# A hybrid encoder block on one core: gate and up's block products take high and low activations as one operand, two weight sums come by adding DMAs, and up's halves are folded one tile per work item

## The chip, the core and the metric

The kernel runs on one core of a Trainium2 chip. TensorE (PE in the profile; PEld is its weight load) multiplies matrices, VectorE (DVE), ScalarE (ACT) and GpSimd (POOL) work on elements, and DMA queues move data between HBM and the core's memory SBUF; SP issues most of them, POOL the others. Matmul results lie in eight banks of PSUM. The engines run side by side and wait for each other by semaphores; each works through its own instructions in order. The metric is the device time of one run, in microseconds (us), with every input in HBM at the start and the output there at the end. All of it is one program.

## The reference

An encoder block for 512 tokens of width 2048: a norm, an input projection, Fourier mixing for one half of the heads and spatial gating for the other, an output projection, then a SwiGLU feed-forward network of width 5632, each with a residual, and a final norm. The change lies in the feed-forward network:

```python
D_MODEL = 2048
SEQ = 512
D_FF = (-(-8 * D_MODEL // (3 * 256))) * 256
...
    for l in range(DEPTH):
        ...
        x = x + jnp.concatenate([y_f, y_g], axis=-1) @ w_out[l]
        h2 = rmsnorm(x, norm_ffn[l])
        x = x + (jax.nn.silu(h2 @ w_gate[l]) * (h2 @ w_up[l])) @ w_down[l]
    return rmsnorm(x, norm_final)
```

All inputs are float32.

## The kernel before

**Products of two halves.** The matmuls take float32r, a rounded float32, so every operand is split in two such tiles: hi is the value rounded (a copy by ScalarE, L173), lo is what the rounding left (value minus hi, by VectorE, L174). A product of two operands is then three matmuls, hi by hi, hi by lo and lo by hi, added up in PSUM.

**Stages.** Input projection and mixing first, then the output projection, then the feed-forward network: 4 of the 44 tiles of 128 ffn features by plain units (GateUp), 32 by block products (Block), the last 8 by plain units again, mixed with the products of the down projection (Product, Last), and at the end the last quarter of the down projection with the final norm.

**Block products.** Two neighbouring ffn tiles, p, are one Matrix for gate (named gb with its p) and one for up (upb). Its weights are four blocks of 1024 columns, 11, 12, 21 and 22 (half of the 2048 inputs, one or the other ffn tile). The tokens are halved as well (H = 256). By Strassen's scheme in Winograd's form the four products of halves are seven instead of eight. Each of the seven is a Block item with number i; sums of weights (Block.sums) and sums of activations (forms, made once in Forms) go in, and sums of the products come out (Block.out). The seven come in the order

```python
    ORDER = (1, 6, 2, 7, 5, 4, 3)
```

An item's matmuls are eight times (one for each of 8 input tiles j) the three of mm3b, each with 128 weight columns as the loaded operand and 256 tokens as the streamed one, all into one half of a PSUM bank:

```python
    def mm3b(ps, lhs, rhs, first, last):
        mm(ps, lhs[0], rhs[0], start=first, stop=False, skip_group_check=True)
        mm(ps, lhs[0], rhs[1], start=False, stop=False, skip_group_check=True)
        mm(ps, lhs[1], rhs[0], start=False, stop=last, skip_group_check=True)
```

There are 16 p, so 32 matrices, 224 items and 5376 such matmuls.

**What sets the order.** In drive the order of each engine is written by hand. While item k's matmuls run, the split of item k + 2 is made (prep), the weight sum of item k + 3 (sums), and the loads of later items are issued (load, by SP; a load waits until its tile's slot is free). Then come late and later, which hold the rest of the work of the one or two items before, then the item's matmuls (run) and the evacuation of its product (out). So VectorE's order in one item is: sum, split, late work, evacuation. A tile hi or lo has three buffers; a split can start when the item before has used its hi for the last time.

**Sums, evacuations and their end.** A matrix has four weight sums on VectorE (L633 to L639, 1024 columns each). Products 1 and 2 are copied out by ScalarE (L666, L670), the five others are added up by VectorE (L668 to L678, 256 columns each), into a tile o of the matrix, [128, 2, 512]. Behind gate's last item o is scaled by the norm (rg, L683), goes through tanh (L692, ScalarE) and becomes gate's silu (L697); behind up's last item, up's o is scaled (L685) and multiplied into gate's (L686), and keep stores the result in HBM (ad, by POOL, L527). The down stage reads it back.

**Slots.** Most tiles of 4 KB a partition come from one pool of 26 slots (slot). The sums of activations (hf) hold 16 of them through the block products; weight blocks go through the other ten. Pool w has three tiles each of raw, hi and lo.

## Time and profile before

| | us |
|---|---|
| three runs | 1849.55, 1850.15, 1850.8 (median 1850.15) |
| profiled execution | 1850.23 |
| its span, first to last instruction | 1848.5 |

The span by stages, cut at the first matmul of each (view by stretches; busy us of each engine, and the mean busy share of the 16 DMA engines):

| stage | us | TensorE | VectorE | ScalarE | POOL | DMA |
|---|---|---|---|---|---|---|
| projections and mixing | 485.74 | 481.27 | 240.92 | 193.65 | 53.02 | 0.36 |
| first 4 ffn tiles of gate and up | 88.52 | 88.36 | 63.66 | 31.68 | 0.84 | 0.37 |
| block products | 648.35 | 646.17 | 555.84 | 270.76 | 8.56 | 0.36 |
| down, last ffn tiles, final norm | 625.89 | 604.14 | 546.95 | 288.90 | 90.09 | 0.75 |

A row of an instruction group reads: line, engine, operation, tiles written and read, their sizes, count, then busy us and the mean ns of one, then the engine's idle time ahead of it and what ended it. A row of the order of time reads: start in us, length, engine, line, operation. The lengths of neighbouring instructions of one engine overlap (a matmul that lasts 0.28 starts 0.12 after the one before), so what one costs in a full queue is read from start to start.

### The profile page before, as it was taken

The numbers are of one execution on the slowest core, as the hardware profiler recorded it, in microseconds if no ns is written. First come the engines' busy times: TensorE is split into PE (matmuls) and PEld (weight loads), VectorE is DVE, ScalarE is ACT, GpSimd is POOL, SyncE is SP. The second block draws the span as 40 slices with busy tenths as digits, with TensorE's granted clock in tenths as the row PEclk, the third lists the DMA queues.
The fourth block names the chain that finished last, engine by engine and source line by source line (L and its number), as shares of the span: only waits on it lengthen the run. The fifth ranks groups of instructions, "written<-read, shape, count | busy, mean of one in ns | idle before, by whom it ended". The sixth has DMA issues, their size and how long they took to land.

```text
span 1848.5 us, 26416 instructions
## 1 busy us (share of the span) xinstructions
PE 1820.0 (98%) x10674; PEld 1614.0 (87%) x10674; DVE 1407.4 (76%) x1683; ACT 785.0 (42%) x1014; POOL 152.5 (8%) x160
## 2 busy tenths in 40 slices
PE   9999999999999999999999999999999999999996
PEld 7888888888888999999999999988888788788785
DVE  7554664333578888888888888889899898899957
ACT  6345533222333444443444444444445455444534
POOL 5001110000000000000000000001111111111104
PEclk9999999999999999999999999999999999999998
DMA  6322224442342343333334333338888878788672
GB/s 244 99 70 95 98 80 137 137 144 95 116 175 86 111 140 115 116 133 107 104 117 137 113 124 128 138 126 205 205 220 206 211 197 208 177 224 210 119 248 111
DMA packets 75577, 269.18 MB, mean 146 GB/s; under 512 B 8768, under 2 KB 8896, under 8 KB 75456
## 3 DMA queue, kind: packets, MB, share of 16 engines
q1 hardware_dynamic: 59616, 209.83, 33.7%
q0 software_dynamic: 15840, 57.68, 15.2%
q8 instruction: 83, 1.36, 0.3%
q14 instruction: 38, 0.31, 0.0%
HBM read 206.66 MB, written 60.82 MB: 145 GB/s over the span
## 4 chain that ended last, share of the span: by engine, by line
PE 89%; DVE 7%; issue 2%; ACT 1%; DMA 0%; POOL 0%; SPq 0%; ACTq 0%; DVEq 0%
PE upb L702 6%; PE upb L700 6%; PE upb L701 6%; PE gb L702 6%; PE gb L701 6%; PE gb L700 6%; PE d L790 5%; PE d L791 5%; PE d L789 5%; PE o L87 3%; PE o L85 3%; PE o L86 3%; PE g L87 2%; PE g L86 2%; PE g L85 2%; PE up L87 2%
## 5 line engine op out<-in xcount | busy, mean ns | idle before, releaser
L790 PE MATMUL d<-lo_d,X 128*128 128x512 f32 x560 | 219.4, 392 | 4.0 <-DVE lo_d L174 4.0
L789 PE MATMUL d<-hi_d,X 128*128 128x512 f32 x560 | 218.1, 389 | 2.4 <-DVE c L812 2.4
L791 PE MATMUL d<-hi_d,X 128*128 128x512 f32 x560 | 218.1, 389 | 0.0
L173 ACT CAST hi_d<-w 128x1024 fp32r<-128x1024 f32 x140 | 147.4, 1053 | 152.2 <-PE d L791 45.7
L174 DVE TENSOR_TENSOR lo_d<-w,hi_d 128x1024 fp32r<-128x1024 f32 x140 | 170.8, 1221 | 28.2 <-ACT hi_d L173 28.1
L173 ACT CAST hi_gb<-w_gb 128x1024 fp32r<-128x1024 f32 x112 | 117.5, 1049 | 150.0 <-PE upb L701 43.7
L173 ACT CAST hi_upb<-w_upb 128x1024 fp32r<-128x1024 f32 x112 | 117.5, 1050 | 135.4 <-PE gb L701 46.6
L174 DVE TENSOR_TENSOR lo_upb<-w_upb,hi_upb 128x1024 fp32r<-128x1024 f32 x112 | 136.8, 1221 | 37.3 <-ACT hi_upb L173 37.3
L174 DVE TENSOR_TENSOR lo_gb<-w_gb,hi_gb 128x1024 fp32r<-128x1024 f32 x112 | 136.7, 1221 | 34.4 <-ACT hi_gb L173 34.4
L702 PE MATMUL gb<-hf,lo_gb 128*128 128x256 f32 x512 | 145.0, 283 | 0.5 <-DVE lo_gb L174 0.5
L701 PE MATMUL gb<-hf,hi_gb 128*128 128x256 f32 x512 | 145.0, 283 | 0.4 <-DVE hf L174 0.4
L700 PE MATMUL gb<-hf,hi_gb 128*128 128x256 f32 x512 | 144.9, 283 | 0.0
L700 PE MATMUL upb<-hf,hi_upb 128*128 128x256 f32 x512 | 144.9, 283 | 0.0
L701 PE MATMUL upb<-hf,hi_upb 128*128 128x256 f32 x512 | 144.9, 283 | 0.0
L702 PE MATMUL upb<-hf,lo_upb 128*128 128x256 f32 x512 | 144.9, 283 | 0.0
L790 PEld LDWEIGHTS d<-lo_d,X 128*128 128x128 f32 x560 | 105.1, 188 | 30.8 <-DVE lo_d L174 9.3
L789 PEld LDWEIGHTS d<-hi_d,X 128*128 128x128 f32 x560 | 105.1, 188 | 25.1 <-ACT hi_up L173 2.0
L791 PEld LDWEIGHTS d<-hi_d,X 128*128 128x128 f32 x560 | 105.1, 188 | 21.3
L80 DVE TENSOR_TENSOR lo_o<-raw_o,hi_o 128x1024 fp32r<-128x1024 f32 x32 | 39.2, 1226 | 102.4 <-ACT hi_o L79 102.4
L700 PE MATMUL gb<-h2hi,hi_gb 128*128 128x256 f32 x384 | 108.8, 283 | 0.8 <-ACT t_gb L666 0.8
L702 PE MATMUL gb<-h2hi,lo_gb 128*128 128x256 f32 x384 | 108.8, 283 | 0.5 <-DVE lo_gb L174 0.5
L700 PE MATMUL upb<-h2hi,hi_upb 128*128 128x256 f32 x384 | 108.7, 283 | 0.0
(322 smaller groups left out, 4981.3 us busy)
## 6 DMA issues: line engine op xcount, KB each, us to landing
w<-in_w_down SPq DMA_DIRECT2D x80, 512.0 KB, 5.7
cd<-c POOLq DMA_DIRECT2D x80, 512.0 KB, 7.2
w_gb<-in_w_gate SPq DMA_DIRECT2D x64, 512.0 KB, 4.1
w_upb<-in_w_up SPq DMA_DIRECT2D x64, 512.0 KB, 4.4
raw_o<-in_w_out SPq DMA_DIRECT2D x32, 512.0 KB, 3.5
raw_g<-in_w_gate SPq DMA_DIRECT2D x24, 512.0 KB, 6.6
raw_up<-in_w_up SPq DMA_DIRECT2D x24, 512.0 KB, 6.8
ac<-ad SPq DMA_DIRECT2D x20, 512.0 KB, 3.6
```

The costliest lines, as they stand in the source:

```text
L80: nc.vector.tensor_sub(lo[:, c], raw[:, c], hi[:, c])
L85: mm(ps, lhs[0], rhs[0], start=first, stop=False)
L86: mm(ps, lhs[0], rhs[1], start=False, stop=False)
L87: mm(ps, lhs[1], rhs[0], start=False, stop=last)
L173: nc.scalar.copy(dst[0], src)
L174: nc.vector.tensor_sub(dst[1], src, dst[0])
L700: mm(ps, lhs[0], rhs[0], start=first, stop=False, skip_group_check=True)
L701: mm(ps, lhs[0], rhs[1], start=False, stop=False, skip_group_check=True)
L702: mm(ps, lhs[1], rhs[0], start=False, stop=last, skip_group_check=True)
L789: mm(p, X[:, 0, j, l], hi, start=j == 0 and not more, stop=False, skip_group_check=True)
L790: mm(p, X[:, 0, j, l], lo, start=False, stop=False, skip_group_check=True)
L791: mm(p, X[:, 1, j, l], hi, start=False, stop=j == 1, skip_group_check=True)
```

## The change

**Matmuls.** hi and lo of the activations now lie side by side in one tile (htile; forms). For each input tile j an item has two matmuls instead of three: the weights' hi streams hi and lo of the activations at once, 512 columns, hi by hi into the left half of the bank and hi by lo into the right; the weights' lo streams hi alone, 256 columns, into the left half. mm3b goes. The two halves of the bank are added when products leave: evacuations are 512 columns wide, and the last steps add halves.

**Weight sums.** Two of the four sums are made by DMA. Tiles w15 and w37 are loaded as 11 and 12 by SP, and POOL then issues a DMA that adds block 12 or 22 from HBM into the tile. Two sums stay on VectorE (L643, L645). A matrix has five slots of weights instead of four. The order of the seven products is BORDER.

**Evacuation.** Products 1, 5 and 2 are copied out by ScalarE, the others are added by VectorE, into two tiles o0 and o1 (one per ffn tile, halves apart). For gate, the halves are added into g (L694, two operations) and g is scaled (L695). For up, fold does it for one ffn tile at a time: add the halves (L703), scale (L704), multiply into g (L706). The first fold stands behind up's last item, the second in late, in the next item. o0, o1 and g take raw buffers of pool w; three raw units behind the stage take slots (early).

```diff
-    hpool = ctx.enter_context(tc.tile_pool(name="h", bufs=2 * KT))
+    hpool = ctx.enter_context(tc.tile_pool(name="h", bufs=KT))
...
     def htile(name):
-        return hpool.tile([P, S], F32R, tag="h", name=name)
+        t = hpool.tile([P, 2, S], F32R, tag="h", name=name)
+        return t[:, 0, :], t[:, 1, :], t
...
-            hi, lo = htile(f"h2hi{c}"), htile(f"h2lo{c}")
+            hi, lo, t = htile(f"h2_{c}")
             g = g_ffn[:, c : c + 1]
             nc.scalar.mul(hi, ps, g)
             nc.vector.scalar_tensor_tensor(lo, ps, g, hi, op0=ALU.mult, op1=ALU.subtract)
-            h2.append((hi, lo))
+            h2.append((hi, lo, t))
...
+    BORDER = (1, 5, 2, 6, 7, 3, 4)
...
                 t = slot(f"hf{j}_{i}", F32R, (P, 2, 2, H))
-                split(x[:, 2 * i : 2 * i + 2, :], (t[:, 0], t[:, 1]))
-                forms[fa, j], forms[fb, j] = ((t[:, 0, k, :], t[:, 1, k, :]) for k in range(2))
+                split(x[:, 2 * i : 2 * i + 2, :], (t[:, :, 0, :], t[:, :, 1, :]))
+                forms[fa, j], forms[fb, j] = t[:, 0], t[:, 1]
             for i, (k, c) in {1: (j, 0), 2: (KT // 2 + j, 0), 4: (KT // 2 + j, H)}.items():
-                forms[i, j] = both(h2[k], slice(c, c + H))
+                forms[i, j] = h2[k][2][:, :, c : c + H]
...
         def load(self):
             m = self.m
-            for k in {1: (11, 12, 22), 6: (21,)}.get(self.i, ()):
+            for k in {1: (11, 15), 5: (22,), 2: (21, 37)}.get(self.i, ()):
                 m.r[k] = slot(f"w{k}_{m.name}")
-                nc.sync.dma_start(m.r[k], m.src[k])
+                nc.sync.dma_start(m.r[k], m.src[{15: 11, 37: 12}.get(k, k)])
+                if k in (15, 37):
+                    nc.gpsimd.dma_start(m.r[k], m.src[12 if k == 15 else 22], accum_op=ALU.add)
 
         def sums(self):
             i, r = self.i, self.m.r
-            add, sub = nc.vector.tensor_add, nc.vector.tensor_sub
-            if i == 1:
-                add(r[12], r[12], r[22])
-            elif i == 6:
-                add(r[11], r[11], r[12])
-            elif i == 7:
-                add(r[21], r[21], r[11])
-            elif i == 5:
-                sub(r[11], r[11], r[22])
-        def behind(self, y):
-            return isinstance(y, Block) and y.m is self.m and (y.i, self.i) in ((1, 6), (2, 7))
+            if i == 6:
+                nc.vector.tensor_add(r[15], r[15], r[22])
+            elif i == 4:
+                nc.vector.tensor_add(r[21], r[21], r[15])
 
         def prep(self):
             i, r = self.i, self.m.r
-            self.split_weights(r[{1: 11, 6: 11, 2: 21, 7: 12, 5: 11, 4: 21, 3: 22}[i]], f"{self.m.name}_{i}")
+            self.split_weights(r[{1: 11, 5: 15, 2: 21, 6: 15, 7: 37, 3: 22, 4: 21}[i]], f"{self.m.name}_{i}")
 
         def run(self):
             m, i = self.m, self.i
             if i == 1:
-                m.o = slot(f"o_{m.name}", F32, (P, 2, S)) if m.up else wpool.tile([P, 2, S], F32, tag="raw", name=f"o_{m.name}")
-                m.t = small.tile([P, 3, H], F32, tag="t", bufs=1, name=f"t_{m.name}")
+                m.o = [wpool.tile([P, 2, 2, H], F32, tag="raw", name=f"o{f}_{m.name}") for f in range(2)]
+                m.t = small.tile([P, 2, S], F32, tag="t", bufs=1, name=f"t_{m.name}")
 
             more = i in (2, 3)
-            m.r["ps", i] = m.r["ps", {2: 1, 3: 5}[i]] if more else bank(f"{m.name}_{i}")
-            ps = m.r["ps", i][:, :H]
+            ps = m.r["ps", i] = m.r["ps", {2: 1, 3: 5}[i]] if more else bank(f"{m.name}_{i}")
             for j in range(KT // 2):
                 c = slice(j * P, (j + 1) * P)
-                mm3b(ps, (self.hi[:, c], self.lo[:, c]), forms[i, j], j == 0 and not more, j == KT // 2 - 1)
+                x = forms[i, j]
+                mm(ps, self.hi[:, c], x, start=j == 0 and not more, stop=False, skip_group_check=True)
+                mm(ps[:, :H], self.lo[:, c], x[:, 0, :], start=False, stop=j == KT // 2 - 1, skip_group_check=True)
 
         def out(self):
             m, i = self.m, self.i
-            ps, o = m.r["ps", i][:, :H], m.o
-            m1, u, w = (m.t[:, k, :] for k in range(3))
+            ps = m.r["ps", i]
+            u, w = m.t[:, 0, :], m.t[:, 1, :]
+            def o(f, t):
+                return m.o[f][:, t].rearrange("p a b -> p (a b)")
             if i == 1:
-                nc.scalar.copy(m1, ps)
+                nc.scalar.copy(u, ps)
+            elif i == 5:
+                nc.scalar.copy(o(1, 1), ps)
+            elif i == 2:
+                nc.scalar.copy(o(0, 0), ps)
             elif i == 6:
-                nc.vector.tensor_add(u, ps, m1)
-            elif i == 2:
-                nc.scalar.copy(o[:, 0, :H], ps)
+                nc.vector.tensor_add(u, ps, u)
             elif i == 7:
                 nc.vector.tensor_add(w, ps, u)
-            elif i == 5:
-                nc.vector.tensor_sub(o[:, 1, H:], ps, w)
-            elif i == 4:
-                nc.vector.tensor_add(o[:, 0, H:], ps, w)
+                nc.vector.tensor_sub(o(1, 1), o(1, 1), w)
+            elif i == 3:
+                nc.vector.tensor_sub(o(1, 0), ps, u)
             else:
-                nc.vector.tensor_sub(o[:, 1, :H], ps, u)
-                scale = rg.unsqueeze(1).to_broadcast([P, 2, S])
+                nc.vector.tensor_add(o(0, 1), ps, w)
                 if not m.up:
-                    pgu["o"] = o
+                    g = pgu["o"] = wpool.tile([P, 2, S], F32, tag="raw", name=f"g_{m.name}")
                     pgu["t"] = slot(f"th{m.p}", F32, (P, 2, S))
-                    nc.vector.tensor_mul(o, o, scale)
+                    for f in range(2):
+                        to = g[:, f, :].rearrange("p (a b) -> p a b", b=H)
+                        nc.vector.tensor_add(to, m.o[f][:, :, 0, :], m.o[f][:, :, 1, :])
+                    nc.vector.tensor_mul(g, g, rg.unsqueeze(1).to_broadcast([P, 2, S]))
                 else:
-                    nc.vector.scalar_tensor_tensor(o, o, 0.5, scale, op0=ALU.mult, op1=ALU.mult)
-                    nc.vector.tensor_mul(pgu["o"], pgu["o"], o)
-                    acts[m.p] = pgu["o"]
-                    keep(m.p)
+                    self.fold(0)
+        def fold(self, f):
+            halves = rg.rearrange("p (a b) -> p a b", b=H)
+            x = self.m.o[f][:, :, 0, :]
+            nc.vector.tensor_add(x, x, self.m.o[f][:, :, 1, :])
+            nc.vector.scalar_tensor_tensor(x, x, 0.5, halves, op0=ALU.mult, op1=ALU.mult)
+            to = pgu["o"][:, f, :].rearrange("p (a b) -> p a b", b=H)
+            nc.vector.tensor_mul(to, to, x)
 
         def late(self):
-            if self.i == 3 and not self.m.up:
+            if self.i == 4 and not self.m.up:
                 nc.scalar.activation(pgu["t"], pgu["o"], AF.Tanh, scale=0.5)
+            elif self.i == 4:
+                self.fold(1)
+                acts[self.m.p] = pgu["o"]
+                keep(self.m.p)
 
         def later(self):
-            if self.i == 3 and not self.m.up:
+            if self.i == 4 and not self.m.up:
                 o = pgu["o"]
                 nc.vector.scalar_tensor_tensor(o, pgu["t"], 1.0, o, op0=ALU.add, op1=ALU.mult)
-    def mm3b(ps, lhs, rhs, first, last):
-        mm(ps, lhs[0], rhs[0], start=first, stop=False, skip_group_check=True)
-        mm(ps, lhs[0], rhs[1], start=False, stop=False, skip_group_check=True)
-        mm(ps, lhs[1], rhs[0], start=False, stop=last, skip_group_check=True)
 
...
-            items += [Block(m, i) for i in ORDER]
+            items += [Block(m, i) for i in BORDER]
...
+        items[-1].early = n < 3
...
-    nc = bacc.Bacc("TRN2", target_bir_lowering=False, num_devices=1, dynamic_dma_scratch_size=8192)
+    nc = bacc.Bacc("TRN2", target_bir_lowering=False, num_devices=1, dynamic_dma_scratch_size=4096)
```

What moves on VectorE, at the end of an up and the start of the next gate. A name ends in the pair p, the product's number and a number of the build: lo_gb6_1_6025 is the low half of the weights of product 1 of gate, pair 6; gb6, upb5 in the place of a source are products in PSUM, t their running sums. In the program before, from up's second-last evacuation on:

```order
L676 TENSOR_TENSOR o_upb5_5874<-upb5_4_6029,t_upb5_5875 128x256
L174 TENSOR_TENSOR lo_gb6_6_6056<-w11_gb6_5833,hi_gb6_6_6055 128x1024
L678 TENSOR_TENSOR o_upb5_5874<-upb5_5_5998,t_upb5_5875 128x256
L685 SCALAR_TENSOR_TENSOR o_upb5_5874<-o_upb5_5874,rstdB_101 128x1024
L686 TENSOR_TENSOR o_gb5_5649<-o_gb5_5649,o_upb5_5874 128x1024
L174 TENSOR_TENSOR lo_gb6_2_6094<-w21_gb6_5871,hi_gb6_2_6093 128x1024
L637 TENSOR_TENSOR w21_gb6_5871<-w21_gb6_5871,w11_gb6_5833 128x1024
L639 TENSOR_TENSOR w11_gb6_5833<-w11_gb6_5833,w22_gb6_5837 128x1024
L174 TENSOR_TENSOR lo_gb6_7_6130<-w12_gb6_5835,hi_gb6_7_6129 128x1024
```

And in the changed one, from up's last evacuation on:

```order
L688 TENSOR_TENSOR o0_upb5_5503<-upb5_4_5649,t_upb5_5505 128x512
L703 TENSOR_TENSOR o0_upb5_5503<-o0_upb5_5503 128x2x256
L704 SCALAR_TENSOR_TENSOR o0_upb5_5503<-o0_upb5_5503,rstdB_101 128x2x256
L706 TENSOR_TENSOR g_gb5_5490<-g_gb5_5490,o0_upb5_5503 128x512
L643 TENSOR_TENSOR w15_gb6_5469<-w15_gb6_5469,w22_gb6_5500 128x1024
L176 TENSOR_TENSOR lo_gb6_2_5672<-w21_gb6_5528,hi_gb6_2_5671 128x1024
L703 TENSOR_TENSOR o1_upb5_5504<-o1_upb5_5504 128x2x256
L704 SCALAR_TENSOR_TENSOR o1_upb5_5504<-o1_upb5_5504,rstdB_101 128x2x256
L706 TENSOR_TENSOR g_gb5_5490<-g_gb5_5490,o1_upb5_5504 128x512
L176 TENSOR_TENSOR lo_gb6_6_5703<-w15_gb6_5469,hi_gb6_6_5702 128x1024
L176 TENSOR_TENSOR lo_gb6_7_5730<-w37_gb6_5530,hi_gb6_7_5729 128x1024
```

Before, two operations of 1024 columns stood between up's last evacuation (L678) and the split of product 2. Now the first fold and a sum stand between the last evacuation (L688) and that split, and the second fold stands between it and the split of product 6.

Behind a gate, from its last evacuation to the split of up's product 2, before:

```order
L678 TENSOR_TENSOR o_gb6_6100<-gb6_5_6223,t_gb6_6101 128x256
L683 TENSOR_TENSOR o_gb6_6100<-o_gb6_6100,rstdB_101 128x1024
L174 TENSOR_TENSOR lo_upb6_2_6318<-w21_upb6_6098,hi_upb6_2_6317 128x1024
L637 TENSOR_TENSOR w21_upb6_6098<-w21_upb6_6098,w11_upb6_6059 128x1024
L639 TENSOR_TENSOR w11_upb6_6059<-w11_upb6_6059,w22_upb6_6063 128x1024
```

And now:

```order
L688 TENSOR_TENSOR o0_gb6_5681<-gb6_4_5826,t_gb6_5683 128x512
L694 TENSOR_TENSOR g_gb6_5844<-o0_gb6_5681 128x512
L694 TENSOR_TENSOR g_gb6_5844<-o1_gb6_5682 128x512
L695 TENSOR_TENSOR g_gb6_5844<-g_gb6_5844,rstdB_101 128x1024
L643 TENSOR_TENSOR w15_upb6_5646<-w15_upb6_5646,w22_upb6_5675 128x1024
L176 TENSOR_TENSOR lo_upb6_2_5851<-w21_upb6_5706,hi_upb6_2_5850 128x1024
L176 TENSOR_TENSOR lo_upb6_6_5879<-w15_upb6_5646,hi_upb6_6_5878 128x1024
```

Where one scaling stood, two additions of halves, the scaling and a sum stand now.

POOL's queue in the stage held only one store for each pair before (ad<-o_gb, L527). Now, from pair 5 on:

```order
L638 DMA w15_upb5_5292<-in_w_up 128x1024
L534 DMA ad_3586<-g_gb4_5136 128x1024
L638 DMA w37_upb5_5354<-in_w_up 128x1024
L638 DMA w15_gb6_5469<-in_w_gate 128x1024
L638 DMA w37_gb6_5530<-in_w_gate 128x1024
L638 DMA w15_upb6_5646<-in_w_up 128x1024
```

Each pair has four adding loads now, and the store of a pair (g) stands ahead of the second adding load of the next pair's up, in the one queue.

More of the change, by code (lines that the diff above doesn't have):

```diff
@@ L131, in load_h @@
         xr = xrs[k // 2][:, k % 2, :]
-        hi, lo = htile(f"hhi{k}"), htile(f"hlo{k}")
+        hi, lo, _ = htile(f"h{k}")
         g = g_mix[:, k : k + 1]
@@ L508, in encoder_block @@
     class RawUnit(Item):
+        early = False
         def __init__(self, src, name):
@@ L514, in load @@
         def load(self):
-            self.raw = wpool.tile([P, U], F32, tag="raw", name=f"raw_{self.name}")
+            if self.early:
+                self.raw = slot(f"raw_{self.name}")
+            else:
+                self.raw = wpool.tile([P, U], F32, tag="raw", name=f"raw_{self.name}")
             nc.sync.dma_start(self.raw, self.src)
```

## The prediction

> **What bounds the kernel now.** First I read the page's chain of what ended last, by engine and by line, to see what carries the span.
>
> ```profile
> PE 89%; DVE 7%; issue 2%; ACT 1%; DMA 0%; POOL 0%; SPq 0%; ACTq 0%; DVEq 0%
> PE upb L702 6%; PE upb L700 6%; PE upb L701 6%; PE gb L702 6%; PE gb L701 6%; PE gb L700 6%; PE d L790 5%; PE d L791 5%; PE d L789 5%; PE o L87 3%; PE o L85 3%; PE o L86 3%; PE g L87 2%; PE g L86 2%; PE g L85 2%; PE up L87 2%
> ```
>
> The six lines of the block products (gb, upb) hold 36% of the chain, all on TensorE. So second comes the view by stretches: the stage that the change touches (574.26 to 1222.61, its first and its next stage's first matmul), and a stretch of the down stage to compare with.
>
> ```profile
> core 0: us, PE busy (x) PEld busy (x) DVE busy (x) ACT busy (x) POOL busy (x), PEclk, DMA share, GB/s
> 574.26:1222.61 648.35, 646.17 (x5377) 645.35 (x5376) 555.84 (x583) 270.76 (x307) 8.56 (x16) 1.00 0.36 120
> 1300.00:1700.00 400.00, 396.32 (x1731) 323.44 (x1730) 366.81 (x437) 191.95 (x243) 53.10 (x63) 1.00 0.81 204
> ```
>
> TensorE is never free in the stage, at full granted clock; VectorE is next with 86%. A matmul's own length in the profile (283 ns) overlaps its neighbour's, so the third view is the order of time, for the step from one start to the next, in the stage and at both ends of it:
>
> ```profile
> 504.68 0.39 PE L87 MATMUL up<-h2hi,lo_up 128*128 128x512 f32 x1
> ...
> 574.04 0.39 PE L87 MATMUL up<-h2hi,lo_up 128*128 128x512 f32 x1
> 574.26 0.28 PE L700 MATMUL gb<-h2hi,hi_gb 128*128 128x256 f32 x1
> ...
> 871.25 0.28 PE L700 MATMUL gb<-hf,hi_gb 128*128 128x256 f32 x1
> ...
> 874.13 0.28 PE L700 MATMUL gb<-h2hi,hi_gb 128*128 128x256 f32 x1
> ...
> 1222.49 0.28 PE L702 MATMUL upb<-hf,lo_upb 128*128 128x256 f32 x1
> 1222.62 0.40 PE L85 MATMUL g<-h2hi,hi_g 128*128 128x512 f32 x1
> ```
>
> From 504.68 to 574.04 lie 306 steps of 512 columns, 0.2267 us each. From 871.25 to 874.13, the first matmuls of two neighbouring products, lie 24 steps of 256 columns, 0.120 each. Where the two widths meet the steps are the same (0.22 for the 512 at 574.04, 0.13 for the 256 at 1222.49, in hundredths). The stage has 224 items of 24 matmuls: 5376 x 0.120 = 645.1, and the stretch is 648.35. So 3.2 us of waiting is in it, at its start.
>
> **The change part by part: TensorE.** The two steps differ by 256 columns and 0.1067 us, so 256 columns cost 0.1067; what is left of a step is 0.120 - 0.1067 = 0.0133 us, paid once for each matmul. An item had 8 x 3 x 0.120 = 2.880 us. Now it has 8 x (0.2267 + 0.120) = 2.773. Nothing else goes away: the columns stay, and one fixed share in three goes. 224 x 8 x 0.0133 = **23.9 us less**, if nothing is late.
>
> The Trainium skill, "TensorE: Matmul & The Clock Gate", section "Back-to-back issue gap", gives N / 2.4 + 2.5 ns for a warm matmul, 109 ns for 256 columns; by it 1792 removed matmuls would give only 4.5 us. The rows above speak against it with 120 and 227 ns.
>
> **VectorE's work.** These rows give its prices by width (and ScalarE's for a cast).
>
> ```profile
> L174 DVE TENSOR_TENSOR lo_gb<-w_gb,hi_gb 128x1024 fp32r<-128x1024 f32 x112 | 136.7, 1221 | 34.4 <-ACT hi_gb L173 34.4
> L173 ACT CAST hi_gb<-w_gb 128x1024 fp32r<-128x1024 f32 x112 | 117.5, 1049 | 150.0 <-PE upb L701 43.7 <-DVE w_gb L635 42.3 <-DVE w_gb L639 40.8
> L812 DVE TENSOR_TENSOR c<-d,uw 128x512 f32<-128x512 f32 x40 | 25.7, 684 | 0.0
> L637 DVE TENSOR_TENSOR w_gb<-w_gb,w_gb 128x1024 f32<-128x1024 f32 x16 | 19.6, 1225 | 0.5
> L672 DVE TENSOR_TENSOR t_gb<-gb,t_gb 128x256 f32<-128x256 f32 x16 | 6.8, 426 | 4.9 <-PE gb L702 4.9
> ```
>
> For one gate and its up (14 items): before, 14 splits and 8 sums and 4 final operations at 1.22, and 10 evacuations at 0.42, are 36.0 us against 14 x 2.880 = 40.3. After: 14 splits, 4 sums, the gate's scaling and its silu product at 1.22 (24.5), and at 0.684 eight evacuations of both halves, two subtractions into o1, two additions of halves and six operations of the folds (18 x 0.684 = 12.3): 36.8 us against 14 x 2.773 = 38.8. The four sums that the adding DMAs take over (4.9 us) are more than given back, and VectorE is nearly full. So its queue decides, and where operations overlap counts:
>
> ```profile
> 575.33 0.68 DVE L559 SCALAR_TENSOR_TENSOR s<-up,rstdB 128x512 f32<-128x512 f32 x1
> 576.04 0.69 DVE L560 TENSOR_TENSOR act<-act,s 128x512 f32<-128x512 f32 x1
> 576.65 0.69 DVE L595 TENSOR_TENSOR hr<-h2hi,h2lo 128x512 f32<-128x512 f32 x1
> ```
>
> ```profile
> 860.41 1.22 DVE L685 SCALAR_TENSOR_TENSOR o_upb<-o_upb,rstdB 128x1024 f32<-128x1024 f32 x1
> 861.66 1.22 DVE L686 TENSOR_TENSOR o_gb<-o_gb,o_upb 128x1024 f32<-128x1024 f32 x1
> 862.81 1.22 DVE L174 TENSOR_TENSOR lo_gb<-w_gb,hi_gb 128x1024 fp32r<-128x1024 f32 x1
> ```
>
> An operation that needs the result of the one ahead starts 0.71 (512 wide) or 1.25 (1024) after it; one that doesn't, 0.61 or 1.15. With these steps the 38 operations need some 35 of 38.8 us (20 x 1.15 and 18 x 0.61 to 0.71), so on the whole VectorE keeps up. It does not at two places, where its row of work is longest between a product's end and a split that TensorE needs. Two more views price them: how soon VectorE starts behind a product, and what a late split costs.
>
> ```profile
> 874.34 0.42 DVE L674 TENSOR_TENSOR o_gb<-gb,t_gb 128x256 f32<-128x256 f32 x1 [0.19 <-PE gb L702]
> ```
>
> ```profile
> 1391.34 1.22 DVE L174 TENSOR_TENSOR lo_g<-raw_g,hi_g 128x1024 fp32r<-128x1024 f32 x1
> 1392.19 0.39 PE L86 MATMUL g<-h2lo,hi_g 128*128 128x512 f32 x1
> 1392.61 0.50 PE L87 MATMUL g<-h2hi,lo_g 128*128 128x512 f32 x1
> 1392.95 0.39 PE L85 MATMUL g<-h2hi,hi_g 128*128 128x512 f32 x1
> ```
>
> VectorE started 0.21 after the next product's first matmul (874.13). The split that ended at 1392.56, 0.37 after the matmul ahead of its user, made two steps of 0.76 instead of 0.45, so it cost 0.30: a lo is free until 0.07 after that start.
>
> Behind an up (VectorE's first pair of orders above): 0.21 to the start, the last evacuation 0.71, first fold 0.71 + 0.71 + 0.61, sum 1.15, split 1.15, second fold 0.71 + 0.71 + 0.61, split of product 6 to its end 1.22: 8.50. TensorE needs it after three items, 3 x 2.773 + 0.07 = 8.39. Late by 0.11. The split of product 2 in the middle lands after 5.3, in time for 5.6. Behind a gate (the second pair): 0.21, evacuation 0.71, two additions 0.61 + 0.71, scaling 1.15, sum 1.15, split of product 2 1.22: 5.76 against 2 x 2.773 + 0.07 = 5.62. Late by 0.14. Sixteen pairs: 16 x 0.25 = **4.0 us more**. In the items that follow, VectorE has 1.2 to 3.1 us of work each and catches up, so lateness doesn't add up. The ends of this term are no lateness (0), and no overlap at all (every step 0.71 or 1.25: 8.90 and 6.06, late by 0.51 and 0.44, so 15.2 us).
>
> **ScalarE, loads and queues.** ScalarE copies three products of both halves instead of two of one; even at the 1.05 us of a cast of 1024 this is 3.2 us of a matrix's 19.4, and ScalarE's share of the stage above is 42%. Behind its copies stand the next casts, which need only the sum above to be done. The DMAs, by their time from issue to landing and by queue (packets, MB, share of 16 engines' span):
>
> ```profile
> cd<-c POOLq DMA_DIRECT2D x80, 512.0 KB, 7.2
> w_gb<-in_w_gate SPq DMA_DIRECT2D x64, 512.0 KB, 4.1
> ```
>
> ```profile
> q1 hardware_dynamic: 59616, 209.83, 33.7%
> q0 software_dynamic: 15840, 57.68, 15.2%
> ```
>
> Each matrix gains one plain load and two adding ones. The queues' shares give, for the 0.524 MB of one weight tile, 0.337 x 16 x 1848.5 / 209.83 x 0.524 = 25 us of engine time on SP's queue and in the same way 41 on POOL's, so 32 x 25 + 64 x 41 = 3424, over 16 engines and 648 us a share of 0.33 more: 0.36 becomes 0.69, below the 0.81 of the down stage, where the additions into HBM (cd) run beside VectorE's work already. An added weight waits for a slot, a plain load, POOL and the addition. By the order with its waits, w15's slot is freed 11 items (30 us) before it is split; 4.1 + 7.2 is 11.3. The trace shows no addition into SBUF: it is bounded by the plain 4.1 below and by twice the 7.2 above; I take 7.2, the only adding row, and nothing is paid at either end: 4.1 + 14.4 is still under 30. On POOL the addition for w37 of an up stands behind the store of the last pair, which waits for the second fold; from there 9 items (25 us) are left. The next gate's tile g waits for that same store, 5 items (14 us) later. SP's loads stand in line behind slots only, as before. Tiles that now hold hi and lo together, three raw units in slots, and the halved scratch of POOL's DMAs I cost at nothing: before the stage TensorE's and SP's orders are the same, and even one POOL transfer at a time would pass the down stage, 80 x 7.2 = 576 us in 626 (1222.62 to the end at 1848.5).
>
> **The sum.** The profiled execution took 1850.23 (span 1848.5), 0.08 above the median of the three runs. 1850.23 - 23.9 + 4.0 = **1830.3**. The 3.2 us of waits at the stage's start I leave, since VectorE's work there, the last forms and the first splits, stays.
>
> **The rivals.**
>
> (1) VectorE's queue behind a gate and an up is longer than I worked out, up to no overlap: 15.2 instead of 4.0, so 1841.5, and some us more if it slows beside the DMAs. For it: 36.8 of 38.8. Against: the overlapping starts above.
>
> (2) The change doesn't save what it says: most of the 13 ns belong to the columns, or come back in the mixed steps, and from 2.2 ns a matmul downwards (4.0 us over 1792) the late splits eat it all: 1850. Against: both mixed steps in the rows. By the rule of the Trainium skill's "TensorE: Matmul & The Clock Gate", section "Back-to-back issue gap", it would end in this rival.
>
> (3) Slower: operations on halves that lie 512 apart are slow. Eight of them stand in the two rows of work of a pair (the folds read or write halves). At the price of a full 1024 row each would cost 0.54 more, 8 x 0.54 x 16 = 69 us, so 1899; it decides from 0.16 us an operation (19.9 / 128). Against it a row with operands in pieces beside one without:
>
> ```profile
> L343 DVE SCALAR_TENSOR_TENSOR v<-vt 128x512 f32<-128x512 f32 x8 | 5.9, 740 | 10.9 <-ACT vt L342 10.7
> L392 DVE SCALAR_TENSOR_TENSOR v<-sv,g_sgu,bB 128x512 f32<-128x512 f32 x8 | 5.6, 745 | 0.0
> ```
>
> L392 takes its operands in four pieces and costs 5 ns more.
>
> **How the numbers follow.** Forecast 0.60 (1826 to 1835: lateness of 0 to 9 us); rival (1) 0.18 (1835 to 1846); rival (2) 0.10 (within 3.7 us of before, 0.2%, which is about what a measurement of this kernel can tell from no change); rival (3) and additions that land too late 0.12. The range takes the first two: 1826 to 1846. Faster by over 0.2%: 0.78; within: 0.10; slower: 0.12.
>
> **What would show it.** Right: 1792 fewer matmuls; items of 2.77 us with steps of 0.227 and 0.120; VectorE above 90% in the stage, waits of TensorE for lo alone, at product 2 behind a gate and product 6 behind an up, 0.1 to 0.2 each; DMA share near 0.7. Wrong: a pair of steps above 0.35, operations of L703 to L706 much above 0.69, waits for weights or for g.

## The result, and the profile after

| | us |
|---|---|
| changed kernel, four runs | 1837.7 to 1838.93, median 1838.1 |
| its span in the profiled execution | 1836.1 |
| kernel before, four runs | 1849.55 to 1850.8, median 1850.09 |
| ratio after to before | 0.9936, 95% interval 0.9922 to 0.995 |
| predicted | 1830.3, range 1826 to 1846 |

The kernel is faster by 12.0 us, 0.64%. The forecast was 19.9 us: the sign and the range hold, and the time is 7.8 us above the forecast. The range holds because it took in rival (1)'s band (1835 to 1846), and the experiments below show that rival (1)'s queue is not what put the time there.

The page of the changed kernel, its counts, its two DMA queues and its chain:

```profile
PE 1807.9 (98%) x8882; PEld 1519.1 (83%) x8882; DVE 1418.8 (77%) x1715; ACT 813.4 (44%) x1046; POOL 208.9 (11%) x224
...
q1 hardware_dynamic: 64224, 226.61, 35.5%
q0 software_dynamic: 25056, 91.24, 26.3%
...
PE 89%; DVE 7%; issue 2%; ACT 1%; DMA 1%; POOL 0%; SPq 0%; ACTq 0%; DVEq 0%
PE gb L663 11%; PE upb L663 11%; PE gb L664 6%; PE upb L664 6%; PE d L807 5%; PE d L808 5%; PE d L806 5%; PE o L89 3%; PE o L87 3%; PE o L88 3%; PE up L89 2%; PE up L87 2%; PE up L88 2%; PE g L89 2%; PE g L87 2%; PE g L88 2%
```

TensorE still holds the chain, now through two lines of the block products (L663 the 512-column matmul, L664 the 256-column one). The stage by the view of stretches, from its first matmul to the next stage's, and the same piece of the down stage as before:

```profile
core 0: us, PE busy (x) PEld busy (x) DVE busy (x) ACT busy (x) POOL busy (x), PEclk, DMA share, GB/s
574.30:1209.65 635.35, 633.36 (x3586) 549.92 (x3585) 566.71 (x612) 299.03 (x339) 61.63 (x77) 1.00 0.72 200
1300.00:1700.00 400.00, 396.32 (x1731) 323.39 (x1731) 365.49 (x436) 191.99 (x244) 51.85 (x61) 1.00 0.81 206
```

The stage went from 648.35 to 635.35 us, 13.0 less; the forecast for it was 621.2 + 3.2 + 4.0 = 628.4. So 6.9 of the missing 7.8 us are in this stage, with the clock at 1.00 and TensorE busy all the time. Behind the stage stand 1836.1 - 1209.65 = 626.4 us, 0.6 more than before.

Waits explain only a part of it. From the view of waits (engine and line, what it waited for, us in total, times, longest), first the waits of the matmuls in the whole stage, then those of the weight loads behind its start, from 590 on:

```profile
PE gb L664 <- DVE lo_gb L176: 1.1, 1, 1.1
PE gb L663 <- ACT t_gb L675: 0.9, 1, 0.9
...
PEld gb L664 <- DVE lo_gb L176: 1.0, 5, 0.2
PEld upb L664 <- DVE lo_upb L176: 0.7, 4, 0.2
```

The first two are at the stage's start. The recorded lengths of matmuls overlap, so the nine short waits show at the weight loads only. What is left is the length of the steps themselves. The order of time on TensorE shows the first matmul of neighbouring items in two parts of the stage, and in the middle an item whose low weights came late:

```profile
814.69 0.39 PE L663 MATMUL gb<-h,hi_gb 128*128 128x512 f32 x1
814.92 0.28 PE L664 MATMUL gb<-h,lo_gb 128*128 128x256 f32 x1
815.03 0.39 PE L663 MATMUL gb<-h,hi_gb 128*128 128x512 f32 x1
...
817.46 0.39 PE L663 MATMUL gb<-hf,hi_gb 128*128 128x512 f32 x1
...
820.23 0.39 PE L663 MATMUL gb<-h,hi_gb 128*128 128x512 f32 x1
...
823.01 0.39 PE L663 MATMUL gb<-hf,hi_gb 128*128 128x512 f32 x1
823.27 0.39 PE L664 MATMUL gb<-hf,lo_gb 128*128 128x256 f32 x1
823.50 0.39 PE L663 MATMUL gb<-hf,hi_gb 128*128 128x512 f32 x1
...
825.96 0.40 PE L663 MATMUL gb<-hf,hi_gb 128*128 128x512 f32 x1
...
854.26 0.40 PE L663 MATMUL gb<-h,hi_gb 128*128 128x512 f32 x1
...
857.08 0.40 PE L663 MATMUL gb<-hf,hi_gb 128*128 128x512 f32 x1
...
859.91 0.40 PE L663 MATMUL gb<-h,hi_gb 128*128 128x512 f32 x1
```

From 814.69 three items take 2.77 us each, as forecast. The item at 823.01 has its first low product 0.26 behind the first high one instead of 0.23, and the next step is 0.23 instead of 0.12. From 854.26 on, items of the same sixteen matmuls take 2.82 and 2.83 us, with no wait in them. To see the pattern, here are the times from each item's first matmul to the next one's, worked out from the starts in the trace (us; a row is one gate and its up, seven items each, and its number is the start of the row):

```
574.3   2.810 3.914 5.734 2.833 2.774 2.773 2.773 | 2.774 2.773 2.920 2.773 2.774 2.773 2.773
617.5   2.774 2.773 2.773 2.962 2.831 2.819 2.830 | 2.831 2.819 2.815 2.773 2.774 2.773 2.773
...
775.5   2.819 2.830 2.831 2.787 2.774 2.773 2.773 | 2.774 2.773 2.927 2.773 2.773 2.774 2.773
814.7   2.773 2.774 2.773 2.958 2.830 2.831 2.819 | 2.830 2.831 2.843 2.830 2.820 2.830 2.830
854.3   2.820 2.830 2.830 2.820 2.830 2.830 2.820 | 2.830 2.830 2.836 2.831 2.819 2.830 2.831
893.8   2.819 2.830 2.831 2.819 2.830 2.831 2.819 | 2.830 2.831 2.836 2.831 2.819 2.830 2.831
933.4   2.819 2.830 2.831 2.787 2.774 2.773 2.773 | 2.773 2.774 2.926 2.774 2.773 2.773 2.774
972.6   2.773 2.773 2.774 2.958 2.830 2.831 2.819 | 2.830 2.831 2.842 2.831 2.819 2.830 2.831
```

The alternating stream has **two beats**. In the fast one a pair of matmuls takes 347 ns (230 and 117). In the slow one the pairs take 361, 349 and 350 ns in turn (241 and 120, 236 and 113, 233 and 117), 353.3 on the mean. A beat lasts over many items and over both matrices. It changes at the fourth item of a gate (product 6), and once, in the row of 617.5, at the third of an up (product 2). Added up over the 224 items:

| us | forecast | measured |
|---|---|---|
| 224 items at 2.773 | 621.2 | 621.2 |
| start of the stage (first four items) | 3.2 | 4.2 |
| late low weights | 4.0 | 1.5 (9 items) |
| slow beat | 0 | 8.4 (156 items) |
| stage | 628.4 | 635.3 |

The row of late weights is what nine items took beyond 2.773; 0.2 us of it are slow steps behind five of the waits.

### The profile page after: what moved, and what is told of

Read it like the earlier page. It is cut to its first block, busy times and chain, and to the rows that moved or that the text cites. A ratio compares the mean times of both kernels' runs of the same rounds, so it can differ in the third digit from the quotient of the medians.

```text
span 1836.1 us, 23223 instructions
## 1 busy us (share of the span) xinstructions
PE 1807.9 (98%) x8882; PEld 1519.1 (83%) x8882; DVE 1418.8 (77%) x1715; ACT 813.4 (44%) x1046; POOL 208.9 (11%) x224
## 4 chain that ended last, share of the span: by engine, by line
PE 89%; DVE 7%; issue 2%; ACT 1%; DMA 1%; POOL 0%; SPq 0%; ACTq 0%; DVEq 0%
PE gb L663 11%; PE upb L663 11%; PE gb L664 6%; PE upb L664 6%; PE d L807 5%; PE d L808 5%; PE d L806 5%; PE o L89 3%; PE o L87 3%; PE o L88 3%; PE up L89 2%; PE up L87 2%; PE up L88 2%; PE g L89 2%; PE g L87 2%; PE g L88 2%
## 5 line engine op out<-in xcount | busy, mean ns | idle before, releaser
L663 PE MATMUL gb<-hf,hi_gb 128*128 128x512 f32 x512 | 181.8, 397 | 0.0
L663 PE MATMUL upb<-hf,hi_upb 128*128 128x512 f32 x512 | 181.4, 396 | 0.0
L664 PE MATMUL gb<-hf,lo_gb 128*128 128x256 f32 x512 | 144.3, 282 | 0.0
L664 PE MATMUL upb<-hf,lo_upb 128*128 128x256 f32 x512 | 143.7, 281 | 0.0
L663 PE MATMUL gb<-h,hi_gb 128*128 128x512 f32 x384 | 138.4, 399 | 0.9 <-ACT t_gb L675 0.9
L663 PE MATMUL upb<-h,hi_upb 128*128 128x512 f32 x384 | 137.6, 396 | 0.0
L835 POOL DMA_DIRECT2D cd<-c x80 | 68.8, 860 | 449.6 <-ACT c L825 163.3
L663 PEld LDWEIGHTS upb<-hf,hi_upb 128*128 128x128 f32 x512 | 96.1, 188 | 23.1
L663 PEld LDWEIGHTS gb<-hf,hi_gb 128*128 128x128 f32 x512 | 96.2, 188 | 22.6
```

The lines of the kernel that those rows point to most:

```text
L663: mm(ps, self.hi[:, c], x, start=j == 0 and not more, stop=False, skip_group_check=True)
L664: mm(ps[:, :H], self.lo[:, c], x[:, 0, :], start=False, stop=j == KT // 2 - 1, skip_group_check=True)
L835: nc.gpsimd.dma_start(cd[self.np_, to // 10 - 1, to % 10 - 1], c, accum_op=ALU.add)
```

## The experiments

After this table stood **theory A**: a wait for low weights throws the stream into the slow beat. Against it **B**: the transfers (share 0.72 of the DMA engines, before 0.36) slow TensorE down. And **C**: the alternation falls into the slow beat by itself.

**All high products first.** Product by product, the eight 512s and then the eight 256s:

```diff
             for j in range(KT // 2):
-                c = slice(j * P, (j + 1) * P)
-                x = forms[i, j]
-                mm(ps, self.hi[:, c], x, ...)
-                mm(ps[:, :H], self.lo[:, c], x[:, 0, :], ...)
+                mm(ps, self.hi[:, j * P : (j + 1) * P], forms[i, j], ...)
+            for j in range(KT // 2):
+                mm(ps[:, :H], self.lo[:, j * P : (j + 1) * P], forms[i, j][:, 0, :], ...)
```

> The changed kernel with each item's sixteen matmuls in another order: the eight of 512 columns first, then the eight of 256. Nothing else moves. The low weights are then wanted 8 x 0.227 - 0.227 = 1.6 us later in every item. Theory A (a matmul that had to wait for low weights, 0.15 to 0.19 us at product 6 behind an up, drops the mixed stream into a slower beat: triples of pairs 349, 350 and 361 ns instead of 347 each, which lasts over several matrices): no wait for low weights, no mixed beat, all items at 8 x 0.2267 + 8 x 0.120 = 2.773 us, the stage 621.2 + 4.2 at the start = 625.4 us against 635.35, the kernel about 1828 us. Theory B (the slow steps come from the transfers, now twice the bytes in SBUF per us): the order of the matmuls doesn't matter, items of 2.82 to 2.83 us remain, about 1836 us. Theory C (a 512 step behind a 256 step costs more at times, whatever was waited for): also 1828, and only a kernel without the wait in the old order tells it from A.

Measured: median 1829.18 us (four runs, 1828.58 to 1829.39), ratio to the kernel before 0.9888, interval 0.9875 to 0.9902, which lies wholly below that of the changed kernel. Its stage by the view of stretches, and two of its items in the order of time (eight equal matmuls in a row are one line there):

```profile
573.52:1200.48 626.96, 626.22 (x3585) 550.62 (x3584) 561.20 (x612) 299.41 (x340) 61.64 (x77) 1.00 0.73 202
```

```profile
694.89 2.00 PE L661 MATMUL gb<-hf,hi_gb 128*128 128x512 f32 x8
696.73 1.12 PE L663 MATMUL gb<-hf,lo_gb 128*128 128x256 f32 x8
697.68 2.00 PE L661 MATMUL gb<-h,hi_gb 128*128 128x512 f32 x8
699.52 1.11 PE L663 MATMUL gb<-h,lo_gb 128*128 128x256 f32 x8
700.48 0.86 PE L661 MATMUL gb<-hf,hi_gb 128*128 128x512 f32 x3
```

Every item behind the first three takes 2.793 us (694.89, 697.68, 700.48), with no wait and no slow beat. That is 0.020 more than forecast, because the 512s behind a run of 256s start at 235 ns a step and come down to 227 only towards the end of their run: 224 x 0.020 = 4.5 us. The start of the stage costs 626.96 - 224 x 2.793 = 1.3 us instead of 4.2, and the wait of 1.1 us for low weights in it is gone. This speaks against B: the transfers (0.73) were the same. A and C are still open.

**The merge alone undone.** Three matmuls of 256 columns per block again, all else as in the changed kernel:

```diff
-                mm(ps, self.hi[:, c], x, ...)
+                mm(ps[:, :H], self.hi[:, c], x[:, 0, :], ...)
+                mm(ps[:, H:], self.hi[:, c], x[:, 1, :], ...)
                 mm(ps[:, :H], self.lo[:, c], x[:, 0, :], ...)
```

> The changed kernel with the merge alone undone: three matmuls of 256 columns per product block again (24 per item), the rest of the change as it is. Theory A: items of 24 x 0.120 = 2.880 us throughout, no slower beat since no widths alternate, and the low weights no longer late (an item is 0.107 us longer than the forecast one); stage 645.1 + 4.2 = 649.3 us, the kernel about 1852 us, so the merge as such is worth 14 us and not 24. Theory B (transfers slow TensorE): items above 2.90 us, stage above 650. A rival on the rest of the change (folds, strided operations or adding transfers cost something by themselves): over 1853 us.

Measured: 1849.96 us, ratio to the kernel before 1.0002, interval 0.9993 to 1.0012. Its stage:

```profile
573.80:1221.31 647.51, 645.63 (x5378) 645.21 (x5376) 567.74 (x612) 299.64 (x339) 61.64 (x77) 1.00 0.72 197
```

All items behind the third take 2.880 us, so no low weight is late behind the start, and the share of the transfers is the same 0.72. So with items of this length adding transfers, folds, strided halves and the new order of products cost and bring nothing by themselves; the gain comes with the merge. Whether the merge would gain as much without the others was not tested. It is worth 11.9 us in the changed kernel's order and 20.8 us with the high products first.

**VectorE lightened by the fold.** Theories A and C differ where the order alternates and nothing is late.

```diff
         def fold(self, f):
-            nc.vector.tensor_add(x, x, self.m.o[f][:, :, 1, :])
-            nc.vector.scalar_tensor_tensor(x, x, 0.5, halves, op0=ALU.mult, op1=ALU.mult)
             nc.vector.tensor_mul(to, to, x)
```

> The changed kernel in its own order of matmuls; the two halves of up are not added and not scaled (two VectorE operations of each of the 32 fold calls are left out, so the values of act are others). VectorE then has about 1.4 us less to do before the low weights of product 6 behind an up. Theory A: the low weights of product 6 are in time, the stream never leaves its fast beat of 2.773 us; what is left is the wait at product 2 behind a gate, 16 x 0.15 = 2.4 us; stage 621.2 + 4.2 + 2.4 = 627.8 us, one time about 1830 us. Theories B and C: items of 2.82 to 2.83 us remain in most of the stage, 633 us or more.

Measured: one run of 1836.51 us, stage 633.86. My number was wrong. The slow beat is entered at a late weight, as A says. Its items from the third pair on:

```
655.1   2.773 2.774 2.773 2.773 2.774 2.773 2.773 | 2.774 2.773 2.927 2.773 2.773 2.774 2.773
694.0   2.773 2.774 2.773 2.773 2.774 2.773 2.773 | 2.774 2.773 2.952 2.830 2.830 2.820 2.830
733.3   2.830 2.819 2.830 2.831 2.819 2.830 2.831 | 2.819 2.830 2.847 2.831 2.819 2.830 2.831
```

Product 6 is in time everywhere and never changes the beat. At up's product 2 the first three waits (items of 2.920 to 2.927) leave the beat fast; the fourth (2.952) turns it slow, and it stays so to the end. The fourth wait is no longer than the others: its item's first two steps, from the trace, take 262 + 221 = 483 ns, those of the third 262 + 224 = 486. What its item takes longer are the slow steps behind the wait. So the length of a wait alone doesn't decide.

**Plain loads.** The same order with fewer transfers:

```diff
                 nc.sync.dma_start(m.r[k], ...)
-                if k in (15, 37):
-                    nc.gpsimd.dma_start(m.r[k], ..., accum_op=ALU.add)
```

> The changed kernel without its adding transfers (two per matrix; the sums of weights of products 5, 6, 7 and 4 miss one term each). The transfers of the stage fall by two fifths, VectorE and TensorE do all that they did. Theory A: nothing changes, low weights are late at the same two places, most items at 2.82 to 2.83 us, stage 635 us, one time about 1838 us. Theory B: items of 2.773 us throughout, stage about 627 us, 1830 us.

Measured: one run of 1836.33 us. Its stage:

```profile
574.06:1208.11 634.05, 632.08 (x3585) 548.55 (x3584) 566.68 (x612) 298.85 (x339) 8.57 (x16) 1.00 0.44 150
```

With the share of the transfers down from 0.72 to 0.44 the slow beat has the same steps, is entered at the same product (in the second pair) and takes as large a part (164 items, in the changed kernel 156). The 1.3 us less in the stage come from its start (2.6 us of waits instead of 4.2). B falls.

**No late weights in the alternating order.** The light fold, and gate's tile unscaled:

```diff
-                    nc.vector.tensor_mul(g, g, rg.unsqueeze(1).to_broadcast([P, 2, S]))
```

> The changed kernel's own order of matmuls, with VectorE lightened ahead of both late places: up's halves are neither added nor scaled, and gate's tile is not scaled (the values of act are others). The kernel without the fold's two operations stayed at 2.773 us per item for three matrix pairs, until a wait of 0.18 us at product 2 of the fourth pair, and was slow from there to the end. Theory A (only a wait for low weights puts the mixed stream into the slow beat): no wait is left at either place, so all items behind the first four at 2.773 us, stage 621.2 + 2.7 to 4.2 = 624 to 625.5 us, one time 1826 to 1828 us. Theory C (the mixed order falls into the slow beat by itself, sooner or later): items of 2.82 to 2.83 us appear without a wait ahead of them, stage above 628 us.

Measured: one run of 1828.04 us, stage 625.43. The stretch from the second pair's first matmul to the stage's end:

```profile
617.18:1199.56 582.38, 582.38 (x3362) 513.50 (x3361) 479.86 (x496) 279.40 (x316) 57.58 (x72) 1.00 0.74 204
```

These are 15 pairs, 210 items: 582.38 / 210 = 2.773 us, and no single item is off by more than 0.001. Its low weights were ready 1.28 us or more before their first use. So C falls as worded: left alone, the alternation keeps its fast beat for 582 us, beside transfers at 0.74.

**High products first at the two late places only** (product 6 of gate, product 2 of up), the rest alternating:

```diff
+            if (i, m.up) in ((6, False), (2, True)):
+                ...
+            else:
                 for j in range(KT // 2):
```

> Eight of 512 first and then eight of 256 only in the two items whose low weights are late (gate's product 6, up's product 2); the other twelve items of a pair alternate 512 and 256 as in the changed kernel. Theory A: the two waits are gone, the alternating items stay at 2.773 us and the two at 2.793: stage 621.2 + 32 x 0.020 + 2.7 to 4.2 = 624.5 to 626 us, the kernel about 1828 us, a little under the kernel with all items in that order (1829.2). Against it: if the step from an ordered item to an alternating one shifts the stream as a wait does, items of 2.82 to 2.83 us follow it and the time is 1830 to 1836 us.

Measured: 1836.78 us, ratio 0.9931, interval 0.9919 to 0.9944; stage 634.70. Behind its start no wait is listed in the stage, and each split of low weights ended 0.53 us or more before its first use, yet all alternating items from the first ordered one on take 2.82 to 2.83 us. So a wait isn't needed: a change of pattern puts the stream into the slow beat as well. The warning in the expectation came true, the forecast didn't.

**Low products one and two steps behind.**

```diff
+            n, lag = KT // 2, 1
+            for j in range(n + lag):
+                if j < n:
+                    mm(ps, self.hi[:, j * P : (j + 1) * P], forms[i, j], ...)
+                k = j - lag
+                if k >= 0:
+                    mm(ps[:, :H], self.lo[:, k * P : (k + 1) * P], forms[i, k][:, 0, :], ...)
```

> The alternating order with the low products one step behind: high 0, high 1, low 0, high 2, low 1 up to high 7, low 6, low 7. The low weights are wanted one 512 step, 0.227 us, later, more than the longest wait seen (0.19 us). Theory A: no wait, items of 2.773 us or a little above (each item has one pair of equal neighbours at each end), stage 621.2 + 4 = 625 us, the kernel about 1828 us. If the equal neighbours shift the stream into the slow beat by themselves: items of 2.82 us, stage 635 us, 1838 us.

> The same with the low products two steps behind, so that the low weights are wanted 0.45 us later than in the changed kernel. Theory A: as with one step, about 1828 us, and if one step left a wait of a few hundredths at some items, this one leaves none. If the shift at the ends decides: slow items as with one step.

Measured: one step behind 1836.71 us (ratio 0.993, 0.9917 to 0.9942), stage 635.46, items of 2.818 and 2.822 in turn. Two steps behind 1832.74 us (0.9908, 0.9895 to 0.9922), stage 629.80, items of 2.788, 2.813 and 2.806 in turn. No late weights behind the start of the stage in either (ready 0.35 and 0.53 us ahead, or more); orders with equal neighbours at an item's ends have slower steps without a wait. The forecasts of 1828 were wrong.

**One disturbance, and three, in a stream without late weights.** The kernel of the fifth experiment, with one item form "one step behind" at chosen places:

```diff
+            n, lag = KT // 2, int((m.p, m.up, i) == (6, 0, 1))
```

> The kernel without late weights (up's halves neither added nor scaled, gate's tile not scaled), all 224 items alternating but one: gate's product 1 of the fifth matrix pair has its low products one step behind (a 512 beside a 512 at its start, a 256 beside a 256 at its end). No wait comes with it. Theory A' (alternation keeps whichever beat its phase puts it in; anything that shifts the phase, a wait or two equal neighbours, changes the beat for good): 2.773 us per item up to that product, 2.82 to 2.83 from it to the end of the stage, 167 items x 0.054 = 9 us more than without the shift, stage 634 us, one time about 1837 us. Rival (the slow beat is tied to waits, or an item's disturbance ends with it): 2.773 us on both sides, stage 625 us, 1828 us.

> The same with that item form at three places: gate's product 1 of the fifth, ninth and thirteenth matrix pair. Theory A': the beat may change at each of the three and at no other place, so four stretches of constant beat; if every shift takes a fast stream to the slow beat and leaves a slow one slow, the stage is as with one shift (634 us); if a shift also takes a slow stream back, about 629 us. Rival: 625 us throughout.

Measured: one place 1827.57 us, stage 625.43: the disturbed item took 2.785 us, and the beat stayed fast on both sides. Three places 1833.26 us, stage 631.42: the first left the beat fast, the second turned it slow, the third left it slow. The second one in the order of time, with the first matmuls of the items around it (the disturbed item begins at 888.64 with two 512s):

```profile
885.87 0.40 PE L663 MATMUL upb<-h,hi_upb 128*128 128x512 f32 x1
...
888.64 0.62 PE L663 MATMUL gb<-h,hi_gb 128*128 128x512 f32 x2
...
891.46 0.40 PE L663 MATMUL gb<-hf,hi_gb 128*128 128x512 f32 x1
...
894.29 0.40 PE L663 MATMUL gb<-h,hi_gb 128*128 128x512 f32 x1
...
897.11 0.40 PE L663 MATMUL gb<-hf,hi_gb 128*128 128x512 f32 x1
```

2.77 us before, 2.82 and 2.83 behind, and so for the 111 items to the stage's end. That one disturbance is always enough was wrong. But the first one did change something. In both kernels the pairs behind it take 344 and 350 ns in turn (231 and 113, 233 and 117) where they took 347 each (230 and 117). The mean is the same, so the fast beat has two patterns; the second disturbance of the last kernel met the other pattern than the first. What holds in both kernels: the pattern changed only at a disturbance, and between two of them never.

## Why the prediction was right or wrong

**Right: the mechanism.** The profile has 10674 - 8882 = 1792 matmuls fewer, no wait for added weights or for g, and without the merge there is no gain (second experiment: ratio 1.0002).

**Right in the fast beat: the price of a removed matmul.** The kernel with no late weights kept 2.773 us per item, 0.107 less than 2.880, over 210 items: 13.3 ns for each removed matmul. The steps inside are 230 and 117 ns, not the 227 and 120 of equal neighbours; only their sum came out. The rule that the prediction weighed (the Trainium skill, "TensorE: Matmul & The Clock Gate", section "Back-to-back issue gap": N / 2.4 + 2.5 ns, there the gap of an isolated matmul) would have given 2.5 ns for each removed matmul; among equal neighbours 256 columns took 120.0 and 512 took 226.7, which is N / 2.4 + 13.3 ns in both rows.

**Wrong: "items of 2.773" as the price everywhere.** This is the term of 23.9 us, and it is the step that failed: it measured 23.9 - 8.4 = 15.5. The prediction took the mixed steps from the two places where 512 and 256 meet once, and took a sum of two single steps for the price of a stream. In 156 of 224 items part of the saving came back in the mixed steps, 0.054 us of 0.107 in a slow item. That is what rival (2) named ("come back in the mixed steps"), at half its price in a slow item. One pair in three of the slow beat takes 0.361 us, above the 0.35 that the prediction had named as a sign of being wrong. Nothing alternated in the kernel before, so it could not show the beat, but it did show dearer steps: behind the 256s at 1222.62 the first five 512s took 233, 236, 228, 233 and 231 ns, and the prediction had read only the one step ahead of them. So a bound was due, and the forecast's own 1826 to 1835 had none for it.

**The late low weights: places and sizes right, count wrong.** VectorE's work behind an up, in the order of time of the changed kernel:

```profile
817.68 1.22 DVE L643 TENSOR_TENSOR w_gb<-w_gb,w_gb 128x1024 f32<-128x1024 f32 x1
818.81 1.22 DVE L176 TENSOR_TENSOR lo_gb<-w_gb,hi_gb 128x1024 fp32r<-128x1024 f32 x1
819.95 0.68 DVE L703 TENSOR_TENSOR o_upb<-o_upb 128x512 f32<-128x512 f32 x1
820.67 0.69 DVE L704 SCALAR_TENSOR_TENSOR o_upb<-o_upb,rstdB 128x512 f32<-128x512 f32 x1
821.39 0.69 DVE L706 TENSOR_TENSOR g_gb<-g_gb,o_upb 128x512 f32<-128x512 f32 x1
822.01 2.35 DVE L176 TENSOR_TENSOR lo_gb<-w_gb,hi_gb 128x1024 fp32r<-128x1024 f32 x2
```

The last row is two splits, of products 6 and 7. The first ends at 822.01 + 1.22 = 823.23, that is 8.54 behind the matmul at 814.69; the prediction's sum was 8.50. The first two steps of a late item took 0.14 us more than a pair of the fast beat, at product 6 and at product 2; forecast were 0.11 and 0.14. (The whole item took 0.185 more at product 6, since slow steps followed.) But only nine items had such a wait, not 32: in the slow beat three items take 0.16 us more, and the same chain is then in time. So the term measured 1.5 instead of 4.0 (1.3 for the waits alone), and the slow beat paid for part of itself.

**Small terms.** The start of the stage cost 4.2 instead of the unchanged 3.2; other kernels with the same matmul order there had 2.6 to 4.2, and why was not looked for. Outside the stage 0.6 us came on top; no experiment looked for it.

**Rivals (1) and (3).** VectorE was busy for 566.71 of 635.35 us, 89%, where I expected above 90; its queue overlapped as forecast. The strided folds take the forecast price (last column but the idle time: mean ns):

```profile
L706 DVE TENSOR_TENSOR g_gb<-g_gb,o_upb 128x512 f32<-128x512 f32 x32 | 22.2, 692 | 1.1
L704 DVE SCALAR_TENSOR_TENSOR o_upb<-o_upb,rstdB 128x512 f32<-128x512 f32 x32 | 22.1, 692 | 1.1
L703 DVE TENSOR_TENSOR o_upb<-o_upb 128x512 f32<-128x512 f32 x32 | 22.0, 689 | 0.5
```

**Transfers.** Share 0.72, forecast 0.69. The adding transfers by issue to landing:

```profile
w_gb<-in_w_gate POOLq DMA_DIRECT2D x32, 512.0 KB, 6.1
w_upb<-in_w_up POOLq DMA_DIRECT2D x32, 512.0 KB, 7.5
```

The estimate of 7.2, taken from the additions into HBM, holds for additions into SBUF, and nothing waited for them.

## What to carry to other kernels

Price a mixed stream of instructions by a mixed stream: two steps read at a single boundary don't say what hundreds of alternations cost, and where the trace has none, bound them. When a merge makes a tight engine faster, look for the operand that now comes last; here eight high products ahead of the eight low ones gave the low weights 1.6 us of slack and took the kernel from 1838.1 to 1829.2 us, most of it because the slow beat (8.4 us) has no place in that order. A merged kernel that gains less than its arithmetic can be read item by item: here equal items of unequal length, with no wait in them, showed that the stream itself had two beats, set off by small disturbances.

## What the runs showed of the hardware

- A stream of alternating float32r matmuls of 512 and 256 columns, each with its own weight load, ran here at 346.7 ns or at 353.3 ns a pair, at granted clock 1.00. It kept one beat for up to 582 us and changed it only in an item whose low split ended behind its first matmul, or at a change of pattern.
- The length of a wait doesn't decide alone. Behind the stage's start, where the fast beat met late weights, the first two steps of the item took 483 to 486 ns where it stayed fast (seven times in the changed kernel and the third experiment) and 490 to 494 where it turned slow (five times), but once 483 turned it slow as well.
- The way back goes by a few nanoseconds. In the changed kernel and the one with plain loads, slow items of product 6 whose low split ended 48 to 50 ns behind the item's first matmul turned the beat fast (six of six, in items of 2.787 or 2.788 us); where it ended 54 to 57 ns behind, the beat stayed slow (fifteen of fifteen). That goes together; no run moved that time by itself.
- The steps depend on the neighbours: 227 ns for a 512 among 512s, 230 to 233 in the fast alternation, 232 to 241 in the slow one, and 233 to 236 falling to 227 behind a run of 256s. A 256 took 120 ns among its like and 112 to 120 in the others.
- What sets the beat stays open. The transfers don't (0.44 and 0.72 of the DMA engines, same beats), nor the form of the moving operand (both forms show both beats), nor a wait as such (the orders with equal neighbours were slower with none, and waits of like length left the beat fast and turned it slow).
